# Score products of two attentions: low parts of the keys in full-height tiles with zero rows

## The chip, the cores and the metric

The kernel runs on one core of a Trainium2 chip, as one launch. The metric is the device time of one execution in microseconds. A core has TensorE (PE, matrix products), VectorE (DVE), ScalarE (ACT), GpSimd (POOL) and a queue for transfers (SP).

## What is computed

Two transformer blocks over 512 latent tokens of width 1024 and 256 context tokens, all in float32. Block one has a feed-forward part, then two attentions side by side (a multi-head latent attention, MLA, with 8 heads over all 768 keys, and a neighbourhood attention), a gated merge, and a second feed-forward part. Block two has a chunked mLSTM and a causal window attention side by side, a gated merge, a feed-forward part and a gate. The change concerns the scores of the neighbourhood attention and of the window attention.

Neighbourhood attention: 8 heads of width 64. The 512 queries are a grid of 8 rows by 64 columns, cut into 4 blocks of 16 columns, each block 128 queries. Each query attends in one softmax to the 8 x 32 keys about its block (256 local keys, with a bias table that also masks) and to all 256 context keys:

```python
s_loc = jnp.einsum('bjqhd,bjakhd->bhjqak', q_r, k_b) + bias
s_ctx = jnp.einsum('bjqhd,bkhd->bhjqk', q_r, k_ctx)
p = jax.nn.softmax(jnp.concatenate([s_loc, s_ctx], axis=-1), axis=-1)
```

Window attention: 16 query heads of width 64 share 4 key heads. Each block of 128 queries sees its own and the preceding block of keys (256 columns, 128 for the first block), with a mask and a sink logit per head.

## The kernel before, in words

**Products in parts.** A float32 product is made from operands split into a high part in PE's fast format (float32r) and a low part, the exact rest. A product of weights and activations is high by high, high by low and low by high: three passes of PE. For the two attentions the width of a head is only 64, so both parts of a query stand in one 128-row tile: in `pair_split` (L1135) and in `swa_side` (L1558) the high part has one half of the rows and the low part the other. The high part of the keys, `kh`, stands twice, in both halves. One product of the whole query tile as weights (128 rows) with `kh` gives high by high plus low by high. The second product adds high query by low key. Before, it takes the 64 rows of the query tile that hold the high part as weights and the 64 rows of `kl` that hold this head's low key part; the two heads of a pair lie in the two halves of one `kl` tile. The two products add into the same bank of PSUM.

**Neighbourhood attention** (`na_heads`, L1111): 4 pairs of heads by 4 blocks of queries make 16 units. For a unit, `scores` (L1163) makes for each of two heads four products of 128 queries by 256 keys (local keys and context keys, `kh` and `kl` each), then adds the bias on DVE (L1174), and takes the softmax (L777 on: maximum on DVE, exponential on ACT, reciprocal on DVE, scaling on POOL). `transposes` (L1180) turn the probabilities on PE, and DVE or ACT copies them out of PSUM; `values` (L1192) multiplies them with the values as 64-column weights. The loop (L1213) writes the scores of the next unit between the transposes and the values of the present one. At block 0 of a pair `pair_load` (L1128) starts the transfer of the next pair's queries and keys (`q32`, `k32`, the keys with one buffer); at block 2 `pair_split` makes all the parts for it, `kl` with two buffers.

Beside these 16 units, in steps written alternately by `beside` (L78), runs `mla_out` (L1095): gates (24 products of 512 columns each) and the output product of MLA (12 products), whose result DVE multiplies into `yb` (L1107), which frees the bank.

**Window attention** (`swa_heads`, L1583): 8 pairs of heads by 4 blocks make 32 units. `scores` (L1587) makes for each of two heads two products, 256 columns wide (128 for the first block). The softmax follows with a look-ahead of two units. Beside it runs `swa_side` (L1558): queries, output gates and branch gates (24 products each). The keys are split earlier, in `swa_k` (L1532), beside the mLSTM.

**Order.** The program is written by Tile; a scheduler that works with a simulated timeline fixes the order of instructions on each engine from the order in which they are written, their dependencies and the buffers. On the chip each engine then works through its queue in that order. Weights come by SP in blocks of 512 KB (L94), POOL makes the high part (L103), DVE the low part (L106).

Of the kernel before, what the change touches and what calls it, by code (L numbers as in the profile page):

```python
# [5 lines left out]
F32 = mybir.dt.float32  # L6
# [6 lines left out]
T = 512          # latent tokens  # L13
C = 256          # context tokens
TC = T + C
# [6 lines left out]
# columns of the per-feature vector array  # L22
# [3 lines left out]
# columns of the constant array  # L26
# [5 lines left out]
class Kern:  # L32
    def __init__(self, tc, A, plan):
        self.tc, self.nc, self.A = tc, tc.nc, A
        self.n_dram = 0
        # weights: the order of their use, and how far each step has come
        self.plan, self.log = plan, []
        self.n_use = self.n_split = self.n_dma = 0
        self.w_st, self.w_parts = {}, {}
        self.w_by = "gv"  # the engines of the high and the low part: Pool, vector or scalar  # L40

# [22 lines left out]
    def split(self, hi, lo, src):  # L64
        """hi + lo == src exactly; src in SBUF or PSUM."""
        self.nc.scalar.copy(hi, src)  # L66
        self.nc.vector.tensor_tensor(out=lo, in0=src, in1=hi.bitcast(F32), op=ALU.subtract)
# [10 lines left out]
    def beside(*gens):  # L78
        """Emits generators, given with their numbers of steps, evenly beside one another."""
# [29 lines left out]
    def w(self, name, *idx, c0=0, n=1024, ahead=2):  # L109
        """The next block of weights [128, n], as (hi, lo); splits up to `ahead` blocks more."""  # L110
# [10 lines left out]
    def w_load(self, i):  # L121
        """Starts the load of block i."""
# [4 lines left out]
    def w_ahead(self, i, ahead=2):  # L127
        """Splits up to `ahead` blocks past i, loads up to four more."""
# [14 lines left out]
    def gemm(self, ps, w, xs, c0=0, start=True, stop=True):  # L143
        """ps[128, N] += sum over blocks k of w[:, c0 + 128k ...].T @ xs[k]; xs = (hi, lo) pairs."""
# [8 lines left out]
    def gemms(self, pss, ws, xs):  # L153
        """Several products at once, block k by block k, for an xs that is still being made."""
# [8 lines left out]
    def gemm_tok(self, pss, keys, xs, n, kpc):  # L163
        """Token-major products: pss[i][128 tokens, n] = xs[i]'s tokens @ W; blocks of kpc k each."""
# [27 lines left out]
    def sums_add(self, acc, y, x, g, first, eng):  # L192
        """Per token: adds y^2, (g y) x and (g y)^2 to three sums over features (still one a partition)."""
# [11 lines left out]
    def sums_next(self, put, A, B, C, r):  # L205
        """A = sum over features of (x + r g y)^2, from the sum of x^2 and those above."""
# [6 lines left out]
    def add_normed(self, put, x, y, r, g):  # L213
        """x += y r g."""
# [4 lines left out]
    def next_h(self, put, eng, x, y, r, pre, shift, hh, hl, lo=None):  # L219
        """Parts of h = x r pre + shift. Returns the step that is left for the low part."""  # L220
# [8 lines left out]
    def queue(self):  # L229
        """A function that keeps the instructions given to it in their order, engine by engine."""  # L230
# [12 lines left out]
    def ln_table(self):  # L243
        """Puts a function table in place that has ln and exp."""
# [4 lines left out]
    def ln(self, out, in_, p=None, **kw):  # L249
        """Natural logarithm, after function table p."""  # L250
# [5 lines left out]
    def rstd(self, r, pp, acc, nfeat, pieces=None, p=None):  # L256
        """r = (sum over partitions of acc / nfeat + eps) ** -0.5, on all partitions; function table p."""
# [9 lines left out]
    def setup(self):  # L267
# [22 lines left out]
        # derived per-feature scale columns  # L290
# [5 lines left out]
    def ada_first(self, k, st, put, tp, pp):  # L296
        """Shift, scale of block k of the features, in two steps. Four quarters of the contraction in four
        row groups; a product with ones at the rows of a stream folds them."""
# [19 lines left out]
    def ada_gen(self, tp, pp):  # L318
        """Modulations 2 to 8, one block of features a step, on the vector engine: features on partitions, the
        conditions along the rows. The context takes part in the first three only."""  # L320
# [38 lines left out]
    def ffn1(self):  # L359
# [30 lines left out]
        # shift and scale of one block of features after the other, h, and the first products  # L390
# [44 lines left out]
        def up(f, gh, gl, ss):  # L435
            """Hidden features f of the streams ss."""
# [51 lines left out]
        # the last group: the context's part first, so that its norms run beside the latents' part  # L488
# [7 lines left out]
        def chain(a, b, s):  # L496
            """Residual and next norm of tokens a..b, in steps; ends with the parts of h."""
# [44 lines left out]
        def chain_c():  # L542
            """Residual and next norm of the context, in steps."""
# [50 lines left out]
        # keys and values of the context, and keys of the latents as their features come, beside the norms  # L594
# [13 lines left out]
    def na_kv(self, pp):  # L608
        """Values and keys of the neighbourhood attention to scratch memory. Three steps for three parts of the
        context's keys, one for each block of features of the latents, then the rest."""  # L610
# [39 lines left out]
    def kv_part(self, tp, pp, s):  # L650
        """Compressed keys and values of the latents (s = 0) or the context, normed, in two parts;
        and the rotary key. Three steps of products, then one of the norm."""
# [35 lines left out]
    def rot(self, ps):  # L688
        """Rotary embedding of four 32-row blocks of ps; returns (a, b) with a + b the result."""
# [10 lines left out]
    def mla_proj(self):  # L700
# [10 lines left out]
        # compressed q: gain now, the norm's factor after the next product  # L711
# [19 lines left out]
        # queries  # L731
# [19 lines left out]
        # keys and values  # L751
# [22 lines left out]
    def softmax(self, p, s, tp):  # L774
        """p = softmax along the free axes of s (PSUM)."""
# [14 lines left out]
    def mla_attn(self):  # L790
        """MLA attention, with projections of the other attention beside it."""
# [8 lines left out]
    def cut(self, hi, lo, src):  # L800
        """As split, without the scalar engine; src in SBUF."""
# [3 lines left out]
    def mla_heads(self, tp, pp):  # L805
        """Two heads and 256 queries at a time; the next scores beside the transposes and values."""
# [67 lines left out]
    def na_q(self, pp):  # L874
        """Queries of the neighbourhood attention and gates to scratch memory."""
# [16 lines left out]
    def na_attn(self):  # L892
        """Neighbourhood attention, with the other branch and its gate beside it; then the merge."""
# [88 lines left out]
        def downs(gi, g, a, b):  # L982
            """Tokens a..b of the part of y that group gi brings."""
# [44 lines left out]
        # the last part of y, its norm, the residual, and the next block's h = x * gain (the norm's factor follows  # L1028
        # its products): one half of the tokens beside the products of the other
# [52 lines left out]
    def gate(self, t, w, ps, h, bias=None, r=None):  # L1082
        """t = sigmoid(w.T @ h (r) + 2 bias) as (tanh(z / 2) + 1) / 2."""
# [27 lines left out]
    def na_heads(self, na, on, pp):  # L1111
# [14 lines left out]
        qk = {}  # L1126

# [7 lines left out]
        def pair_split(hp, q, k):  # L1135
            """Per head: queries as high above low part (second head: the other way), keys' high part
            twice; the low parts of both heads' keys."""
            kl = na.tile([128, TC], F32R, tag="kl", name="kl", bufs=2)
            qs, khs = [], []
            for e in range(2):  # L1140
# [7 lines left out]
                nc.vector.tensor_tensor(out=kl[r, :], in0=k[r, :], in1=kh[r, :].bitcast(F32), op=ALU.subtract)  # L1148
                qs.append(qp)
                khs.append(kh)  # L1150
            qk[hp] = qs, khs, kl
# [11 lines left out]
        def scores(hp, j):  # L1163
            qs, kh, kl = qk[hp]
            out = []
            for e in range(2):
                rows = slice(64 * e, 64 * e + 64)
# [3 lines left out]
                for c, sub in ((slice(0, 256), local), (slice(256, 512), lambda t: t[:, T:TC])):  # L1171
                    self.mm(s[:, c], q, sub(kh[e]), stop=False)
                    self.mm(s[:, c], q[rows], sub(kl)[rows], start=False)
# [36 lines left out]
        pair_split(0, *nxt)  # L1210
        cur = scores(0, 0)
        yield 1
        for n, (hp, j) in enumerate(units):  # L1213
# [8 lines left out]
            if j == 2 and hp < 3:  # L1222
                pair_split(hp + 1, *nxt)
            pbs = transposes(cur)
            if n + 1 < len(units):
                cur = scores(*units[n + 1])
# [659 lines left out]
```

## Time and profile before

| | |
|---|---|
| Median of 3 runs | 2535.81 us (2535.79 to 2536.38) |
| Span of the profiled execution, first to last instruction | 2535.5 us |
| Instructions in the span | 31842 |
| PE busy | 2456.4 us (97%), 12360 products |
| DVE busy | 1428.1 us (56%) |
| POOL busy | 818.0 us (32%) |
| ACT busy | 602.6 us (24%) |
| Neighbourhood attention | about 952 to 1092 us of the span |
| Window attention | about 1800 to 1988 us of the span |

The profile is of one execution. Records of PE's products are pipelined: a record's duration includes the way through the array, so consecutive records overlap, and the time that a product holds the engine is read from one start to the next. A share of busy time is a mean over the span. In the view of waits, a line tells which engine and line waited for which, in total, how many times, and the longest.

### The profile page before, as it was taken

How to read it: one execution, taken by the hardware profiler on the slowest of the kernel's cores; microseconds unless marked ns; L12 is line 12 of the kernel's file. 1: busy time of each engine (PE TensorE's matmuls, PEld its weight loads, DVE VectorE, ACT ScalarE, POOL GpSimd, SP SyncE). 2: the span in 40 equal slices, each digit the busy share in tenths (PEclk: the TensorE clock that was granted, in tenths of full speed). 3: DMA queues.
4: the chain of work that ended last, by engine and by line, in shares of the span. 5: the costliest groups of instructions: out<-in, count | busy, mean ns of one | idle time of the engine just before them, and what ended most of it. 6: DMA issues, size and time to landing. Idle time of an engine off the chain costs nothing.

```text
span 2535.5 us, 31842 instructions
## 1 busy us (share of the span) xinstructions
PE 2456.4 (97%) x12360; PEld 2001.6 (79%) x12360; DVE 1428.1 (56%) x2152; ACT 602.6 (24%) x1153; POOL 818.0 (32%) x778
## 2 busy tenths in 40 slices
PE   7999999998999999998999999999999999999997
PEld 4888888987787776776788888777777788888886
DVE  5956555578356447578423338944766545344356
ACT  3210101143223332224111015223533202011023
POOL 2111111336234334355221226725434334212132
PEclk9999999998999999999999999999999999999999
DMA  7444444334322125153332335222222343333332
GB/s 285 158 128 148 128 142 125 126 105 129 131 88 92 55 92 160 61 170 100 95 97 93 101 98 158 84 92 84 80 71 68 117 158 99 100 94 98 99 93 92
DMA packets 97479, 284.67 MB, mean 112 GB/s; under 512 B 10892, under 2 KB 16908, under 8 KB 96176
## 3 DMA queue, kind: packets, MB, share of 16 engines
q1 hardware_dynamic: 87872, 265.86, 32.8%
q10 hardware_dynamic: 9456, 16.78, 2.0%
q8 instruction: 97, 1.59, 0.3%
q14 instruction: 54, 0.44, 0.1%
HBM read 260.32 MB, written 21.50 MB: 111 GB/s over the span
## 4 chain that ended last, share of the span: by engine, by line
PE 85%; DVE 7%; issue 2%; POOL 1%; ACT 1%; DMA 1%; DVEq 0%; POOLq 0%; ACTq 0%
PE mm L59 75%; PE s L59 4%; PE o L59 3%; DVE wlo L106 1%; PE t L853 1%; DVE y L216 1%; PE n L59 1%; PE t L1186 1%; PE q L59 1%; PE pt L1630 1%; DVE acc L190 0%; POOL mqk L1355 0%; DVE t L199 0%; DVE xx L1048 0%; DMA k<-scr 0%
## 5 line engine op out<-in xcount | busy, mean ns | idle before, releaser
L103 POOL TENSOR_SCALAR whi<-wst 128x1024 fp32r<-128x1024 f32 (+4 forms) x387 | 411.7, 1065 | 1334.1 <-PE mm L59 1243.8
L106 DVE TENSOR_TENSOR wlo<-wst,whi 128x1024 fp32r<-128x1024 f32 (+4 forms) x398 | 490.2, 1234 | 288.5 <-POOL whi L103 281.9
L59 PE MATMUL mm<-h2l,whi 128*128 128x512 f32 (+1 forms) x1024 | 354.6, 353 | 3.0 <-DVE h2l L227 3.0
L59 PE MATMUL mm<-h2h,whi 128*128 128x512 f32 (+1 forms) x1024 | 353.4, 354 | 2.4 <-ACT h2h L415 1.9
L59 PE MATMUL mm<-h2h,wlo 128*128 128x512 f32 (+1 forms) x1024 | 353.5, 352 | 2.3 <-DVE wlo L106 2.3
L59 PE MATMUL mm<-gh,whi 128*128 128x512 f32 (+1 forms) x848 | 297.2, 352 | 0.3 <-POOL whi L103 0.3
L59 PE MATMUL mm<-gh,wlo 128*128 128x512 f32 (+1 forms) x848 | 296.4, 351 | 0.7 <-DVE wlo L106 0.7
L59 PE MATMUL mm<-gl,whi 128*128 128x512 f32 (+1 forms) x848 | 296.3, 351 | 0.0
L59 PEld LDWEIGHTS mm<-h2h,wlo 128*128 128x128 f32 x1024 | 194.2, 191 | 30.1 <-DVE wlo L106 3.2
L59 PEld LDWEIGHTS mm<-h2h,whi 128*128 128x128 f32 x1024 | 194.7, 192 | 29.3 <-ACT h2h L415 2.8
L59 PEld LDWEIGHTS mm<-h2l,whi 128*128 128x128 f32 x1024 | 194.5, 192 | 29.5 <-DVE h2l L227 5.0
L59 PEld LDWEIGHTS mm<-gh,wlo 128*128 128x128 f32 x848 | 159.5, 188 | 23.3 <-DVE wlo L106 1.1
L59 PEld LDWEIGHTS mm<-gh,whi 128*128 128x128 f32 x848 | 159.5, 188 | 22.3 <-POOL whi L103 0.8
L59 PEld LDWEIGHTS mm<-gl,whi 128*128 128x128 f32 x848 | 159.7, 188 | 21.7
L59 PE MATMUL mm<-hmh,whi 128*128 128x512 f32 (+1 forms) x432 | 167.1, 398 | 4.0 <-ACT whi L101 4.0
L59 PE MATMUL mm<-hmh,wlo 128*128 128x512 f32 (+1 forms) x432 | 163.0, 390 | 5.4 <-DVE wlo L106 5.4
L59 PE MATMUL mm<-hml,whi 128*128 128x512 f32 (+1 forms) x432 | 161.3, 386 | 0.1
L59 PE MATMUL mm<-hl,whi 128*128 128x512 f32 x352 | 137.9, 392 | 4.3 <-DVE hl L227 4.3
L59 PE MATMUL mm<-hh,wlo 128*128 128x512 f32 x352 | 139.0, 395 | 0.3 <-DVE wlo L106 0.3
L59 PE MATMUL mm<-hh,whi 128*128 128x512 f32 x352 | 137.5, 397 | 0.5 <-POOL whi L103 0.3
L66 ACT CAST gh<-sa 128x512 fp32r<-128x512 f32 (+1 forms) x66 | 36.1, 549 | 276.2 <-DVE sa L456 156.9
L59 PE MATMUL mm<-h4h,whi 128*128 128x512 f32 x256 | 101.2, 395 | 0.0
(414 smaller groups left out, 4429.1 us busy)
## 6 DMA issues: line engine op xcount, KB each, us to landing
wst<-in_f2w SPq DMA_DIRECT2D x60, 512.0 KB, 3.3
ast<-in_w_adaT SPq DMA_DIRECT2D x56, 512.0 KB, 3.3
wst<-in_f1w SPq DMA_DIRECT2D x54, 512.0 KB, 3.4
wst<-in_wup SPq DMA_DIRECT2D x32, 512.0 KB, 3.5
wst<-in_wdn SPq DMA_DIRECT2D x32, 512.0 KB, 3.8
st<-in_w_ada SPq DMA_DIRECT2D x8, 1024.0 KB
wst<-in_wg SPq DMA_DIRECT2D x16, 512.0 KB, 3.2
wst<-in_w2g SPq DMA_DIRECT2D x16, 512.0 KB, 3.6
```

The lines of the kernel that those rows point to most:

```text
L59: ins = self.nc.tensor.matmul(out=out, lhsT=lhsT, rhs=rhs, start=start, stop=stop)
L66: self.nc.scalar.copy(hi, src)
L103: self.nc.gpsimd.tensor_scalar(out=hi[:, :n], in0=st[:, :n], scalar1=1.0, scalar2=0.0, op0=ALU.mult, op1=ALU.add)
L106: e.tensor_tensor(out=lo[:, :n], in0=st[:, :n], in1=hi[:, :n].bitcast(F32), op=ALU.subtract)
L216: put(v.tensor_tensor(out=y, in0=y, in1=r, op=ALU.mult))
L853: nc.tensor.transpose(pt[:, i:i + 128], P[2 * hp + e, 2 * half + q][:, 128 * (2 * c + kk):128 * (2 * c + kk) + 128], self.ident)
L1186: nc.tensor.transpose(pt[:, c], ps[e][:, c], self.ident)
L1630: nc.tensor.transpose(pt[:, kk, e, :], p[:, e, 128 * kk:128 * kk + 128], self.ident)
```

## The change

For both attentions the second score product now uses the whole query tile (128 rows) as weights, as the first does, and the low part of each head's keys stands in a 128-row tile of its own, whose other half is zero. The zero rows face the low part of the query, so that the sum is that of before.

In the neighbourhood attention there are two such tiles, one for each head of a pair (`klz`, one buffer each), whose zero halves are set once by POOL, ahead of the loop; before there were two buffers of one tile for both heads. As the tiles are used by all pairs, the step that makes the low parts is taken out of `pair_split` and is written behind the scores of the next unit, at block 2 of a pair: the scores of block 3 are the last that read the old low parts. In the window attention the low parts have four tiles instead of two, and POOL sets the zero halves in `swa_k`. Comments and docstrings were also taken out.

```diff
         qk = {}
+        klz = [na.tile([128, TC], F32R, name=f"klz{e}") for e in range(2)]
+        for e in range(2):
+            nc.gpsimd.memset(klz[e][64 - 64 * e:128 - 64 * e, :].bitcast(F32), 0.0)
...
         def pair_split(hp, q, k):
-            kl = na.tile([128, TC], F32R, tag="kl", name="kl", bufs=2)
-            qs, khs = [], []
+            qs, khs, src = [], [], {}
...
-                nc.vector.tensor_tensor(out=kl[r, :], in0=k[r, :], in1=kh[r, :].bitcast(F32), op=ALU.subtract)
                 qs.append(qp)
                 khs.append(kh)
-            qk[hp] = qs, khs, kl
+            qk[hp] = qs, khs
+
+            def low():
+                for e in range(2):
+                    r = slice(64 * e, 64 * e + 64)
+                    nc.vector.tensor_tensor(out=klz[e][r, :], in0=k[r, :], in1=khs[e][r, :].bitcast(F32),
+                                            op=ALU.subtract)
+
+            return low
...
         def scores(hp, j):
-            qs, kh, kl = qk[hp]
+            qs, kh = qk[hp]
...
                     self.mm(s[:, c], q, sub(kh[e]), stop=False)
-                    self.mm(s[:, c], q[rows], sub(kl)[rows], start=False)
+                    self.mm(s[:, c], q, sub(klz[e]), start=False)
...
-        pair_split(0, *nxt)
+        pair_split(0, *nxt)()
...
             if j == 2 and hp < 3:
-                pair_split(hp + 1, *nxt)
+                low = pair_split(hp + 1, *nxt)
             pbs = transposes(cur)
             if n + 1 < len(units):
                 cur = scores(*units[n + 1])
+            if j == 2 and hp < 3:
+                low()
             yield 1
             values(hp, j, po, pbs)
...
     def swa_k(self, sw, at, pp, h, r, swk):
...
-            kl = sw.tile([128, T], F32R, name=f"kl{m}")
             for e in range(2):
                 kh = sw.tile([128, T], F32R, name=f"kh{2 * m + e}")
+                kl = sw.tile([128, T], F32R, name=f"kl{2 * m + e}")
                 rws, oth = slice(64 * e, 64 * e + 64), slice(64 - 64 * e, 128 - 64 * e)
+                nc.gpsimd.memset(kl[oth, :].bitcast(F32), 0.0)
                 self.split(kh[rws, :], kl[rws, :], t[rws, :])
                 nc.scalar.copy(kh[oth, :], t[rws, :])
-                swk.append((kh, kl[rws, :]))
+                swk.append((kh, kl))
...
                 self.mm(s[:, e, :w], q[:, c], kh[:, ck], stop=False)
-                rws = slice(64 * (m // 2 % 2), 64 * (m // 2 % 2) + 64)
-                self.mm(s[:, e, :w], q[rws, c], kl[:, ck], start=False)
+                self.mm(s[:, e, :w], q[:, c], kl[:, ck], start=False)
```

## Rows read from the trace of the kernel before

**Rows 1.** The page, its first lines: span, and busy time of engines.

```profile
span 2535.5 us, 31842 instructions
PE 2456.4 (97%) x12360; PEld 2001.6 (79%) x12360; DVE 1428.1 (56%) x2152; ACT 602.6 (24%) x1153; POOL 818.0 (32%) x778
```

**Rows 2.** Busy time by stretch: length, PE, PEld, DVE, ACT, POOL, granted clock, DMA.

```profile
952.00:1092.00 140.00, 138.73 (x740) 99.33 (x738) 87.57 (x163) 38.54 (x90) 49.62 (x62) 0.96 0.38 121
1800.00:1988.00 188.00, 188.00 (x960) 138.37 (x959) 122.81 (x306) 66.71 (x212) 76.54 (x108) 1.00 0.24 74
966.00:975.40 9.40, 9.24 (x23) 6.61 (x24) 9.27 (x15) 2.12 (x5) 8.50 (x8) 0.50 0.63 182
```

**Rows 3.** Waits from 930 to 1100 us: total, times, longest.

```profile
DVE pb L786 <- PE t L1186: 18.0, 10, 4.4
...
PE mm L59 <- DVE yb L1107: 1.2, 1, 1.2
```

**Rows 4.** Waits from 1795 to 1990 us.

```profile
DVE t L1087 <- PE mm L59: 22.2, 13, 2.7
```

**Rows 5.** PE's timeline, a run of eight score products: start, duration, operation, shape.

```profile
1806.71 0.28 PE L59 MATMUL s<-kh,q 128*128 128x256 f32 x1
1806.92 0.38 PE L59 MATMUL s<-kl,q 64*128 64x256 f32 x1
1807.24 0.38 PE L59 MATMUL s<-kh,q 128*128 128x256 f32 x1
...
1809.11 0.51 PE L59 MATMUL mm<-hmh,wlo 128*128 128x512 f32 x1
1809.46 0.40 PE L59 MATMUL mm<-hmh,whi 128*128 128x512 f32 x1
1809.69 0.40 PE L59 MATMUL mm<-hml,whi 128*128 128x512 f32 x1
```

**Rows 6.** PE's timeline, last stage: first and last of 31 products of 256 columns.

```profile
2508.52 0.28 PE L59 MATMUL mm<-h5h,whi 128*128 128x256 f32 x1
...
2511.92 0.28 PE L59 MATMUL mm<-h5h,whi 128*128 128x256 f32 x1
```

**Rows 7.** PE's timeline, MLA scores: two products with the same weights.

```profile
925.93 0.34 PE L59 MATMUL s<-kh,qh 96*128 96x384 f32 x1
926.10 0.33 PE L59 MATMUL s<-kl,qh 96*128 96x384 f32 x1
```

**Rows 8.** PE's timeline, a high-part score beside a product with 64 weight columns.

```profile
1036.87 0.39 PE L59 MATMUL s<-kh,q 128*128 128x256 f32 x1
1037.19 0.54 PE L59 MATMUL o<-pb,nv 128*64 128x128 f32 x5
```

**Rows 9.** PE's timeline, eight transposes and the score behind them.

```profile
1062.49 1.09 PE L1186 MATMUL t<-cst,p 128*128 128x128 f32 x8
1063.34 0.37 PE L59 MATMUL s<-kh,q 128*128 128x256 f32 x1
```

**Rows 10.** Instructions on the score operands, whole span: duration ns min/median/max, starts.

```profile
L59 PEld LDWEIGHTS s<-kh,q x128: 185/187/330, 951.6 to 1980.5; 128*128 128x128 f32 x128
...
L59 PE MATMUL s<-kl,q x128: 282/382/580, 953.3 to 1980.8; 64*128 64x256 f32 x112, 64*128 64x128 f32 x16
...
L1148 DVE TENSOR_TENSOR kl<-k,kh x8: 940/1107/1357, 950.8 to 1025.4; 64x768 fp32r<-64x768 f32 x8
```

**Rows 11.** PE's timeline, a group of four score products of 128 columns.

```profile
1813.84 0.22 PE L59 MATMUL s<-kh,q 128*128 128x128 f32 x1
...
1815.09 0.40 PE L59 MATMUL mm<-hml,whi 128*128 128x512 f32 x1
```

**Rows 12.** DVE's timeline, 956 to 967 us: in brackets idle time before, and releaser.

```profile
963.00 0.55 DVE L1146 CAST kh<-k 64x768 fp32r<-64x768 f32 x1 [6.01 <-DMA k<-scr]
...
965.33 0.69 DVE L1107 TENSOR_TENSOR yb<-yb,mm 128x512 f32<-128x512 f32 x1
```

**Rows 13.** Groups of POOL's instructions, whole span: busy us, mean ns.

```profile
L1324 POOL MEMSET rowp<- 36x2560 f32 x1 | 2.2, 2228 | 0.0
```

More of the change, by code (lines that the diff above doesn't have):

```diff
@@ L1163, in scores @@
         def scores(hp, j):
-            qs, kh, kl = qk[hp]
+            qs, kh = qk[hp]
             out = []
             for e in range(2):
-                rows = slice(64 * e, 64 * e + 64)
                 s = self.bank(pp, "s", 3)
```

## Prediction

> **What bounds the kernel now.** I read the page's busy shares first. TensorE (PE) is busy for 97% of a span of 2535.5 us [rows 1]; the median of the runs is 2535.81 us, so the profiled execution lies 0.3 us below it, and I make the sum against 2535.5 and add 0.3. A busy PE is not a PE at its peak, so I then read the two stretches that the change touches: the neighbourhood attention, 952 to 1092 us, and the window attention, 1800 to 1988 us. In the first PE counts as busy for 138.73 of 140 us, in the second for all of 188; DVE for 87.57 and 122.81 us, which is 63% and 65% [rows 2]. The waits agree: in the first stretch PE's only long wait for another engine's result is 1.2 us, and DVE waits 18.0 us for transposes alone [rows 3]; in the second DVE waits 22.2 us for products [rows 4]. Others wait for PE, so an instruction that PE issues sooner should move the end.
>
> The last view is PE's timeline, read by distances from start to start, as the recorded durations overlap. The reader should see the following in a run of eight score products [rows 5]: high keys, low keys, high keys, low keys, each 256 columns wide, and they start 0.31 to 0.32 us apart (first pair 0.21). Full-array products of the same width in the last stage start 30 steps from 2508.52 to 2511.92, 0.113 us apart [rows 6]. Two differences stand beside one another: the score products change from 128 weight rows to 64 and back, the others don't. MLA's scores change nothing in shape; there two products in a row with the same weights, 384 columns wide, start 0.17 us apart [rows 7], so neither using the weights twice nor adding into one bank costs such a gap. I take the 0.2 us beyond 0.113 as the price of changing shape. It shows in a third place: a product that goes over to 64 weight columns starts 0.32 us after a 256-column score [rows 8], while a score follows transposes without it (eight transposes take 0.85 us, 0.106 each [rows 9]).
>
> **The change part by part.**
> *Low-part products go from 64 to 128 weight rows.* Their number stays 128, of them 112 of 256 columns and 16 of 128 [rows 10]. The price is read from whole groups. In the run of eight the first score starts at 1806.71 and the second product behind the group at 1809.46; a product there takes 0.23 (1809.46 to 1809.69), so the group holds PE for 1809.46 - 0.23 - 1806.71 = 2.52 us [rows 5]. Eight at 0.113 would be 0.90. Saved: 1.62 for four low products, 0.40 each. For 128 columns, a group of four holds it 1815.09 - 0.23 - 1813.84 = 1.02 us [rows 11]; four at 0.106, taking the transposes' step, would be 0.42; saved 0.30 for each low product. Sum: 112 x 0.40 + 16 x 0.30 = 49.6 us. Less where the shape changes anyhow: counted over the timeline of the two stretches, a low product stands directly beside a 64-column product 5 times, and a few low products stand beside one another; together some 7 changes of 0.2, so 1.4. That leaves 48 us of PE time. Bounds for the new step: below, 0.107 us (256 columns at 2.4 GHz, what 0.113 already nearly is), above, 0.17 as in the wider MLA scores; at 0.17 the 256 score products would lose 256 x 0.057 = 15 us of it. I take 0.113, the row with the same width.
>
> *What of it lies on the path.* Nearly all, as PE leads in both stretches, but three pieces come off.
> (a) Start of the neighbourhood attention. DVE waits 6.01 us until 963.00 for the second pair's keys, casts them, and only then, at 965.33, multiplies the product that frees a bank for PE [rows 12]; PE waits 1.2 us for that [rows 3]. That transfer doesn't go faster, so two units' saving ahead of it, 2 x 1.62 = 3.2 us, turns into waiting. DVE loses nothing there, as the low parts come behind it.
> (b) The low parts now have one buffer instead of two. For each of the three later pairs two subtractions (median 1.11 us [rows 10]) must stand between the last scores of a pair and the first of the next. A unit is 140 / 16 = 8.75 us, some 7.1 after the saving; 2.2 us fit. They are queued on DVE in order, with the mask additions and the evacuations behind them, and these hold up softmax and PE's banks. Lower bound 0 (an earlier place of the same work could even relieve the DVE before), upper bound, if the unit before gives no cover, 3 x 2.2 = 6.7. I take 2, nearer the lower end as DVE still has slack. The transfer of the next pair's keys waits for the subtraction that reads the same buffer, on SP's queue with the weight loads behind it; four units lie between, about 28 us, against the longest wait for such keys of 6.01, so I put it at nothing unless the order is bad.
> (c) DVE does the same work in less time: 87.57 of about 115 us and 122.81 of about 164, some 76%. Nothing of it is longer, but its queue is in order, and products wait for its evacuations. Bounds: 0, and 15 us if a third of the saving is lost to it; I take 3, since DVE now waits for PE and not the reverse.
>
> *Zeros.* POOL sets two tiles of 64 x 768 ahead of the first stretch and four of 64 x 512 beside the mLSTM. The set of 36 x 2560 took 2.23 us, 0.87 ns a column [rows 13]; that makes 0.67 us each and 0.45 us each, 3.1 us in all. POOL is busy 49.62 of 140 us in the first stretch [rows 2]; the work hides unless splits of weights stand behind it at a bad place, then up to 3 us. I take 0.
>
> Sum: 48 - 3.2 - 2 - 3 = 40 us; 2535.5 - 40 + 0.3 = 2495.8, about 2496 us.
>
> **A rule against it.** The run of full-array products starts every 0.113 us while a weight load is recorded at 0.187 us [rows 6, 10], so the load lies beside the product before it. The Trainium skill, "TensorE: Matmul & The Clock Gate", section "Part 3: Packing small matmuls", says that a weight load overlaps a running product only when their row groups differ. With every score on all rows, that would expose each load: 0.113 + 0.187 = 0.30 us a step, as before, and the change would bring nothing. This is a rival below; the trace doesn't agree with the rule here. The same skill, "TensorEngine Tiling (Array Packing)", section "Key Properties", says that changing the tiling mode drains the engine, which agrees with the 0.31 us.
>
> **The rivals.**
> 1. *Other engines take up a good part (25%).* The hand-over in (b) and the queue in (c) cost PE waits, and after a wait the clock can fall: from 966 to 975.4 us, behind the 1.2 us wait, the granted clock was 0.50, the 1.2 GHz level, for 9.4 us [rows 2, 3], which costs 4.7 us of work. With the upper bounds 6.7 and 15 in place of 2 and 3 the gain is 48 - 3.2 - 6.7 - 15 = 23; with a new fall of the clock about 19: 2512 to 2517 us. For it: DVE's share rises by 12 points in both stretches. Against: PE doesn't wait for DVE in the second at all.
> 2. *The stretch at half clock goes (10%).* The order in the first stretch shifts so that the wait at 965 us or its sequel vanishes: 48 + 4.7 + 1.2 - 2 = 52 less, 2484 us; without losses at (b) and (c) 2482.
> 3. *Nothing changes (4%).* The gap isn't the shape, or loads show as the rule has it: 2535 us. Against it stand the 0.113 and 0.17 us steps.
> 4. *Slower (3%).* One mechanism: the single low-part buffer at the three hand-overs. If each holds PE for x us and drops the clock as at 966, the cost is 3 (x + 4.7); it eats the 45 us that are left after (a) once x passes 10.3. That takes keys arriving late behind the subtraction that frees their buffer, a 6.01 us wait [rows 12], four casts of 0.55 and two subtractions of 1.11: 10.4 us, just at the point, with no other products to fill PE. PE has products of the other branch beside it, so it is unlikely; with x = 12 it would give 2541 us.
>
> **How the numbers follow.** The forecast of 2496 us, with 2489 to 2506 as its own spread, has 58%; the rivals as above. Faster by over 0.2% (5.1 us, about what a measurement of this kernel can tell from no change): 0.93; within it 0.04; slower 0.03. The range reaches from rival 2 to most of rival 1: 2484 to 2515.
>
> **What would show it.** In the changed profile: no product with 64 weight rows; high and low score products about 0.113 us apart, and a run of eight near 0.9 us; the stretch of the first attention about 20 us shorter, that of the second about 23; PE's busy share near 97% still. Wrong would be: steps of 0.2 us or more inside the groups (price of the step), PE waits on the low-part subtraction at three places (b), DVE above 85% with PE waiting on its evacuations (c), a granted clock of 0.50 at new places, or a stretch elsewhere that grew because instructions were placed in another order.

## The result, and the profile after

The changed kernel takes 2496.86 us in the median (2496.39 to 2496.94, 4 runs), the kernel before 2535.8 us (2533.8 to 2536.38): a ratio of 0.9844, 95% interval 0.9832 to 0.9856. The forecast was 2496.0 us. The total came out as written; its parts didn't all, and the experiments sort them.

The first lines of the page of the changed kernel, which answer to [rows 1]:

```profile
span 2495.1 us, 31838 instructions
PE 2408.0 (97%) x12360; PEld 1985.4 (80%) x12360; DVE 1426.9 (57%) x2152; ACT 599.0 (24%) x1151; POOL 828.7 (33%) x784
```

As many products as before, 48.4 us less PE busy; DVE and ACT are as they were, POOL has 10.7 us more, of which 3.7 are the zeros. PE's timeline of the changed kernel, a run of eight score products (start, duration, operation, shape), which answers to [rows 5]:

```profile
958.35 0.29 PE L59 MATMUL s<-kh,q 128*128 128x256 f32 x1
958.48 0.29 PE L59 MATMUL s<-klz,q 128*128 128x256 f32 x1
...
959.33 0.40 PE L59 MATMUL mm<-h2l,whi 128*128 128x512 f32 x1
959.56 0.40 PE L59 MATMUL mm<-h2h,wlo 128*128 128x512 f32 x1
```

The group holds PE for 959.56 - 0.23 - 958.35 = 0.98 us, where before it was 2.52. So a low product saves 0.385 us; 0.40 was forecast from a step of 0.113, and the step came out at 0.12.

The two profiled spans differ by 40.4 us, the medians by 38.9. Where the 40.4 us lie is read from first starts. The lines of instructions by tile (in ns minimum/median/maximum, then first and last start, in us) of the kernel before, and then of the changed one:

```profile
L59 PE MATMUL s<-kh,q x128: 218/382/580, 951.9 to 1980.5; 128*128 128x256 f32 x112, 128*128 128x128 f32 x16
...
L59 PE MATMUL mm<-onh,whi x32: 394/394/501, 1095.5 to 1116.9; 128*128 128x512 f32 x32
...
L59 PE MATMUL q<-mqk,mqk x32: 270/432/697, 1689.8 to 1776.4; 128*128 128x512 f32 x8, 128*128 128x384 f32 x8, 128*128 128x256 f32 x8, 128*128 128x128 f32 x8
...
L59 PE MATMUL mm<-sbh,whi x64: 388/394/506, 1991.3 to 2073.2; 128*128 128x512 f32 x64
```

```profile
L59 PE MATMUL s<-kh,q x128: 220/283/415, 949.9 to 1940.5; 128*128 128x256 f32 x112, 128*128 128x128 f32 x16
...
L59 PE MATMUL mm<-onh,whi x32: 394/394/502, 1079.5 to 1100.9; 128*128 128x512 f32 x32
...
L59 PE MATMUL q<-mqk,mqk x32: 270/432/697, 1671.8 to 1758.4; 128*128 128x512 f32 x8, 128*128 128x384 f32 x8, 128*128 128x256 f32 x8, 128*128 128x128 f32 x8
...
L59 PE MATMUL mm<-sbh,whi x64: 388/394/505, 1950.9 to 2032.8; 128*128 128x512 f32 x64
```

From the first score of the neighbourhood attention to the first product behind it (`onh`) is the **first stretch**: 1095.5 - 951.9 = 143.6 us before, 129.6 after, 14.0 less. From the mLSTM's first product (`mqk`) to the first product behind the window attention (`sbh`) is the **second stretch**: 301.5 before, 279.1 after, 22.4 less. The other 4.0 us lie outside of both.

The waits of the changed kernel (total, times, longest) in the first stretch:

```profile
DVE kh L1148 <- DMA k<-scr: 16.0, 3, 9.3
...
PE mm L59 <- DVE yb L1107: 6.7, 1, 6.7
...
PE o L59 <- DVE pb L786: 3.7, 3, 3.0
```

and about the second:

```profile
DVE t L1087 <- PE mm L59: 10.6, 11, 1.9
```

In the first stretch, the wait of 1.2 us in [rows 3] has become 6.7, and a second one of 3.0 us is new. In the second, DVE still waits for PE, 10.6 us in place of the 22.2 of [rows 4]. DVE's timeline shows where the first stretch's waits come from (in brackets idle time before, and releaser):

```profile
963.57 0.55 DVE L1148 CAST kh<-k 64x768 fp32r<-64x768 f32 x1 [9.29 <-DMA k<-scr]
...
989.23 0.55 DVE L1148 CAST kh<-k 64x768 fp32r<-64x768 f32 x1 [4.82 <-DMA k<-scr]
```

and PE's, what follows from them:

```profile
966.70 0.77 PE L59 MATMUL mm<-omh,whi 128*128 128x512 f32 x1 [6.74 <-DVE yb L1107]
...
994.34 0.90 PE L59 MATMUL o<-pb,nv 128*64 128x128 f32 x5 [3.04 <-DVE pb L786]
```

DVE stands at the cast of keys that haven't come: of the second pair until 963.57, as in [rows 12], and of the third until 989.23. (In the kernel before DVE also stood 4.57 us at the third pair's keys, and PE didn't wait for what stood behind them.) Behind the casts on its queue are the multiplication and the copy that PE needs. Behind both waits the granted clock was 0.50, the 1.2 GHz level, for 3.2 and 6.2 us, together the 9.4 us of before [rows 2]:

```profile
966.60:969.80 3.20, 3.10 (x7) 2.51 (x8) 3.14 (x6) 1.36 (x3) 2.58 (x3) 0.50 0.39 132
994.30:1000.50 6.20, 6.16 (x28) 5.32 (x29) 6.14 (x14) 2.03 (x5) 2.05 (x3) 0.50 0.18 57
```

(busy time by stretch; columns as in [rows 2]).

### The profile page after: what moved, and what is told of

Read it like the earlier page. It is cut to its first block, busy times and chain, and to the rows that moved or that the text cites. A ratio compares the mean times of both kernels' runs of the same rounds, so it can differ in the third digit from the quotient of the medians.

```text
span 2495.1 us, 31838 instructions
## 1 busy us (share of the span) xinstructions
PE 2408.0 (97%) x12360; PEld 1985.4 (80%) x12360; DVE 1426.9 (57%) x2152; ACT 599.0 (24%) x1151; POOL 828.7 (33%) x784
## 4 chain that ended last, share of the span: by engine, by line
PE 47%; DVE 5%; issue 2%; ACT 1%; POOL 1%; DMA 0%; DVEq 0%; ACTq 0%; POOLq 0%
PE mm L59 44%; DVE wlo L106 1%; PE n L59 1%; PE o L59 1%; PE s L59 1%; PE q L59 1%; PE pt L1641 1%; POOL whi L103 0%; DVE xx L1048 0%; DVE mqk L1367 0%; ACT L245 0%; DVE hml L1267 0%; POOL mqk L1365 0%; DVE y L216 0%; DVE xz L1721 0%
## 5 line engine op out<-in xcount | busy, mean ns | idle before, releaser
L59 PEld LDWEIGHTS mm<-gh,whi 128*128 128x128 f32 x848 | 159.5, 188 | 22.4 <-POOL whi L103 0.8
```

What stands on the lines that cost most here:

```text
L59: ins = self.nc.tensor.matmul(out=out, lhsT=lhsT, rhs=rhs, start=start, stop=stop)
```

## The experiments

The table has the median, the ratio to the kernel before in the same set of runs, and from each profile the two stretches and the rest of the span, in us.

| kernel | median | ratio, 95% interval | first | second | rest |
|---|---|---|---|---|---|
| before | 2535.8 | | 143.6 | 301.5 | 2090.4 |
| changed | 2496.86 | 0.9844 (0.9832 to 0.9856) | 129.6 | 279.1 | 2086.4 |
| E1 window part only | 2511.68 | 0.9901 (0.9884 to 0.9918) | 145.2 | 279.2 | 2086.7 |
| E2 neighbourhood part only | 2520.6 | 0.9936 (0.9919 to 0.9953) | 126.4 | 301.5 | 2090.7 |
| E3 mirrored order | 2517.5 | 0.9921 (0.9906 to 0.9936) | 135.3 | 290.9 | 2092.0 |
| E4 keys twice | 2497.04 | 0.9842 (0.9827 to 0.9857) | 126.8 | 279.2 | 2087.4 |
| E5 early keys | 2501.27 | 0.9862 (0.9848 to 0.9875) | 130.6 | 279.1 | 2089.5 |
| E6 early keys, queries | 2493.89 | 0.9832 (0.9818 to 0.9845) | 123.6 | 279.1 | 2090.5 |
| E7 before, early keys | 2538.76 | 1.0013 (1.0004 to 1.0022) | 145.8 | 301.5 | 2088.7 |
| E8 low parts made twice | 2493.64 | 0.9831 (0.9818 to 0.9845) | 126.4 | 279.1 | 2085.9 |
| E9 one pair loaded | 2486.53 | 0.9796 (0.9779 to 0.9812) | 116.6 | 279.2 | 2090.1 |
| E10 pairs by ScalarE's queue | 2493.11 | 0.9825 (0.9810 to 0.9839) | 122.1 | 279.1 | 2089.3 |
| E11 the same, early | 2494.01 | 0.9828 (0.9813 to 0.9843) | 124.1 | 279.2 | 2090.3 |
| E12 values by ScalarE's queue | 2493.47 | 0.9824 (0.9809 to 0.9838) | 124.9 | 279.1 | 2088.1 |

Two things stand out before any single run. The second stretch has three values, for the three ways of its scores, and is the same to 0.1 us within each. The rest of the span goes from 2085.9 to 2092.0 with no relation to what was edited, though apart from POOL's two sets of zeros for `klz` (0.73 us each) and the issue of early loads no edit lies there; so of the first profile's 40.4 us the 4.0 outside the stretches lie within that scatter.

**E1, the window part alone** (`swa_k` and `swa_heads` of the changed kernel in the kernel before):

```diff
-                swk.append((kh, kl[rws, :]))
+                swk.append((kh, kl))
...
-                self.mm(s[:, e, :w], q[rws, c], kl[:, ck], start=False)
+                self.mm(s[:, e, :w], q[:, c], kl[:, ck], start=False)
```

> Only the window attention's part of the change. Theory (each low product loses two changes of shape, 0.40 us at 256 columns and 0.30 at 128, and the window attention has no other loss): 22 to 24 us less than before, about 2512 to 2514 us, with the neighbourhood stretch as before. Rival (the gain in the window attention depends on the first attention's new order, or the 4 us that the changed profile gains outside the two stretches belong to the window part): 18 us or less, or 26 us and more.

2511.68 us, 24 less than before: the theory holds. In the profile 22.3 us of it lie in the second stretch, as in the changed kernel, and the first is no shorter.

**E2, the neighbourhood part alone** (the changed kernel with `swa_k` and `swa_heads` as before):

```diff
-                swk.append((kh, kl))
+                swk.append((kh, kl[rws, :]))
```

> Only the neighbourhood attention's part. Theory (25 us of PE time saved there, about 11 given back to waits for the pairs' keys): 13 to 16 us less than before, about 2520 to 2523 us, with PE waits of about 6.7 us and 3 us in that stretch. Rival (the two parts share the loss, each part alone gives its full 24): 2512 us or less.

2520.6 us, 15 less: the time is the theory's, and by the medians the two parts add up (24 + 15 = 39). PE waits 7.1 us at the same place. But the second wait, which the theory counted in, is at most 0.5 us here, and the first stretch is 126.4 us, 3.2 shorter than in the changed kernel, though the same lines of the program make it. DVE stands 2.26 us at the third pair's keys, in place of 4.82; so the 3.0 us wait of the changed kernel is a matter of how late those keys land.

**E3, mirrored order.** The kernel before, its 64-row products untouched, in the order high, low, low, high:

```diff
-                for c, sub in ((slice(0, 256), local), (slice(256, 512), lambda t: t[:, T:TC])):
-                    self.mm(s[:, c], q, sub(kh[e]), stop=False)
-                    self.mm(s[:, c], q[rows], sub(kl)[rows], start=False)
+                ctx = lambda t: t[:, T:TC]
+                self.mm(s[:, 0:256], q, local(kh[e]), stop=False)
+                self.mm(s[:, 0:256], q[rows], local(kl)[rows], start=False)
+                self.mm(s[:, 256:512], q[rows], ctx(kl)[rows], stop=False)
+                self.mm(s[:, 256:512], q, ctx(kh[e]), start=False)
```

(and in the same way for the two heads of a unit of the window attention).

> The kernel before, with 64-row low products as they were, in mirrored order: high, low, low, high instead of high, low, high, low, so two changes of shape in a group of four instead of four. Theory (the price is the change of shape, 0.2 us each): a group of four takes about 0.4 us less, 64 groups some 25 us of PE time, of which the neighbourhood part loses some to the wait for keys: 2512 to 2520 us. Rival (a product with 64 weight rows is dear by itself, whatever stands beside it): no change, 2533 to 2538 us.

2517.5 us, 18 less. PE's timeline of this kernel:

```profile
1814.74 0.28 PE L59 MATMUL s<-kh,q 128*128 128x256 f32 x1
1814.95 0.50 PE L59 MATMUL s<-kl,q 64*128 64x256 f32 x2
1815.38 0.39 PE L59 MATMUL s<-kh,q 128*128 128x256 f32 x1
1815.61 0.39 PE L59 MATMUL mm<-hmh,whi 128*128 128x512 f32 x1
```

A group of four takes 1815.61 - 1814.74 = 0.87 us, with two changes of shape. With four it took half of 2.52, so 1.26, and in the changed kernel, with none, half of 0.98, so 0.49. Each pair of changes costs 0.38 to 0.39 us, 0.19 for one, with products of 256 columns. As E3 has as many 64-row products as the kernel before, the price is shown to be that of the change of shape, and not of the 64 rows.

The records of the weight loads (PEld) show where the time goes. In the kernel before, each load in the run of eight starts with its own product, those of [rows 5] at 1806.92 and 1807.24:

```profile
1806.92 0.18 PEld L59 LDWEIGHTS s<-kl,q 64*128 64x128 f32 x1 [0.25 <-issue]
1807.23 0.19 PEld L59 LDWEIGHTS s<-kh,q 128*128 128x128 f32 x1
```

In the changed kernel it starts with the product before, so that the load for the product at 958.48 lies beside the one that starts at 958.35:

```profile
958.36 0.19 PEld L59 LDWEIGHTS s<-klz,q 128*128 128x128 f32 x1
958.48 0.19 PEld L59 LDWEIGHTS s<-kh,q 128*128 128x128 f32 x1
```

Counted over the trace of the kernel before, all 200 score products that directly follow a product of another shape have a load that starts with them, to 0.005 us. In the changed kernel 252 follow one of the same shape, and 249 of these have their load earlier, by 0.12 us in the median. So a change of shape costs about one weight load (0.18 to 0.19 us) that no longer lies beside the product before. The Trainium skill, "TensorEngine Tiling (Array Packing)", section "Key Properties", says that a change of the tiling mode drains the engine; a load that waits for the product before is in keeping with that, and the price here is 0.19 us.

**E4, two buffers for the pairs' keys** in the changed kernel:

```diff
-            k = na.tile([128, TC], F32, tag="k32", name="k32")
+            k = na.tile([128, TC], F32, tag="k32", name="k32", bufs=2)
```

> The changed kernel, with two buffers for the keys of a pair as they come from memory instead of one. Theory (the two PE waits in the neighbourhood stretch, 6.7 and 3.0 us, and the half clock behind them, come from DVE standing at a cast whose keys are late because their only buffer was freed late): both go, 10 to 14 us less than the changed kernel, 2483 to 2488 us. Rival (DVE is simply full there, and the wait moves to its next instruction): within 3 us of the changed kernel, 2494 to 2499 us.

2497.04 us: the theory falls as far as the time goes. The second wait is gone, the first stays:

```profile
PE mm L59 <- DVE yb L1107: 6.5, 1, 6.5
```

DVE still stands 9.0 us at the second pair's keys. With the second buffer their transfer was issued at 949.15 in place of 951.10, and they landed at 962.89 in place of 963.57: the buffer was not what made them late. The third pair's keys were issued at 966.27 in place of 983.34, and for that wait the theory was right.

**E5 and E6, earlier transfers.** In E5 the second pair's keys are loaded ahead of the biases and values, in E6 its queries too (both with two key buffers). E6's edit, beside the second buffer:

```diff
         nxt = pair_load(0)
+        nxt1 = pair_load(1)
         bias_load(0)
...
-                nxt = pair_load(hp + 1)
+                nxt = pair_load(hp + 1) if hp else nxt1
```

> The changed kernel with two key buffers, and the transfer of the second pair's keys written ahead of the biases and values instead of behind the first scores. Theory (the PE wait of about 6.5 us at the start of the neighbourhood stretch is DVE standing at the cast of keys that wait behind the biases and values on the queue, and the half clock follows from it): the wait shrinks to under 1 us, 6 to 9 us less than the changed kernel, 2488 to 2491 us. Rival (the transfers at that place are as much as the memory queue can carry, so the biases or values become late instead): within 2 us of the changed kernel, 2495 to 2499 us.

> As the run before, with the second pair's queries moved ahead too. Theory: if DVE or POOL stand at the queries once the keys are there, this is another 1 to 3 us less than with early keys alone; if the keys alone were late, the same within 1.5 us. Rival (a buffer of the shared tag is held longer, so that the gates' first step waits): slower than early keys alone by 2 us or more.

E5 takes 2501.27 us; neither theory nor rival had that. It is not shown to be slower than the changed kernel: the intervals overlap, and in the profiles only 1.0 us of the difference lies in the first stretch. The wait at the cast is gone, but POOL now stands at the queries (its timeline), and PE at the transposes of the probabilities that POOL scales (the waits):

```profile
969.24 1.81 POOL L1152 TENSOR_SCALAR q<-q 64x512 fp32r<-64x512 f32 x2 [9.77 <-DMA q<-scr]
```

```profile
PE t L1201 <- POOL p L782: 8.3, 1, 8.3
```

E6 takes that away, 2493.89 us, 7 less than E5, where 1 to 3 were expected. The wait moves to the low parts of the second pair. Its keys are there, but the subtractions stand on DVE's queue behind the casts of the third pair's keys, which haven't come (DVE's timeline, then the waits):

```profile
978.73 0.55 DVE L1148 CAST kh<-k 64x768 fp32r<-64x768 f32 x1 [7.82 <-DMA k<-scr]
...
980.22 0.95 DVE L1157 TENSOR_TENSOR klz<-k,kh 64x768 fp32r<-64x768 f32 x1
```

```profile
PE s L59 <- DVE klz L1157: 5.9, 2, 5.0
```

**E7, early keys in the kernel before** (the edit of E5: two key buffers, the second pair's keys ahead of the biases).

> The kernel before with the same early keys. Theory (there the same wait was 1.2 us, with half the clock for 9.4 us behind it, 4.7 us of work): 3 to 6 us less than before, 2530 to 2533 us. Rival (the fall of the clock has another cause than the wait): 1 us less at most.

2538.76 us, 3 more than before: the theory falls. Here too the wait only moved, to POOL's scaling (3.7 us), and the half clock came with it: 0.63 in the mean from 970 to 980 us.

**E8, the low parts twice.** The changed kernel with the hand-over's subtractions written twice for the three later pairs:

```diff
             if j == 2 and hp < 3:
                 low()
+                low()
```

> The changed kernel with the low parts of the three later pairs subtracted twice, so six subtractions more on DVE, 6.6 us of its time, at the hand-overs. Theory (the hand-over is covered by the unit beside it): 0 to 2 us more than the changed kernel, 2496 to 2499 us. Rival (the hand-over lies on the path, as its upper bound of 6.7 us had it): 5 to 8 us more, 2502 to 2505 us.

2493.64 us, no slower; by the profiles it is 3.2 us shorter in the first stretch, which has the large wait but not the second one:

```profile
PE mm L59 <- DVE yb L1107: 7.6, 1, 7.6
```

So the hand-over is covered, as the theory had it: E2 and E4, which have the first wait alone too, have first stretches of 126.4 and 126.8 us with the subtractions made once, and E8 has 126.4. That it came out shorter than the changed kernel is not explained by the edit; the order of instructions moved, and DVE no longer stood at the third pair's keys.

**E9, one pair's data for all.** The changed kernel with one load of queries and keys:

```diff
-            q = self.np_.tile([128, T], F32, tag="t", name="q32", bufs=3)
+            q = na.tile([128, T], F32, tag="q32", name="q32")
...
             if j == 0 and hp < 3:
-                nxt = pair_load(hp + 1)
+                pass
```

> The changed kernel without the transfers of the three later pairs' queries and keys: all pairs use those of the first pair (left out: the loads of queries and keys of heads 2 to 7, so those heads' scores are of heads 0 and 1). All arithmetic stays. Theory (at the start of the neighbourhood stretch PE waits for what stands behind late transfers of pairs; each earlier load only handed the wait to the next late one): no PE wait over 1 us from 950 to 1000 us, the stretch 7 to 10 us shorter than in the changed kernel, 2486 to 2490 us. Rival (DVE and POOL have too much to do there, transfers or not): PE waits of 5 us or more remain, 2493 us or more.

2486.53 us, within the theory's range. No wait of PE in the stretch is longer than 0.5 us, and the clock stays whole. Busy time by stretch (columns as in [rows 2]), of the changed kernel and then of this one:

```profile
950.00:1070.00 120.00, 110.22 (x706) 89.25 (x706) 82.20 (x155) 36.13 (x85) 47.68 (x59) 0.94 0.39 120
```

```profile
950.00:1070.00 120.00, 118.66 (x786) 95.02 (x785) 91.17 (x170) 39.86 (x92) 48.12 (x61) 1.00 0.43 137
```

DVE is busy for 91.17 us there, 9 more than in the changed kernel in the same time, and PE isn't held up: it was not DVE's load that made PE wait, it was the transfers. (E9 also takes the queries out of the buffers that they share with the gates; no run separates that.) The first stretch is 13.0 us shorter than in the changed kernel, more than the 7 to 10 expected; 9.8 are the two waits, and the half clock (9.4 us at 0.50, 4.7 of work) is more than the rest.

**E10 to E12, another queue.** E10: two key buffers, and the pairs' loads issued by ScalarE's queue. E11: the same, the second pair early. E12: E6, with the local values issued by ScalarE's queue.

```diff
-            nc.sync.dma_start(out=q, in_=self.naq[hp])
-            nc.sync.dma_start(out=k, in_=self.nak[hp])
+            nc.scalar.dma_start(out=q, in_=self.naq[hp])
+            nc.scalar.dma_start(out=k, in_=self.nak[hp])
```

> The changed kernel with two key buffers and the transfers of the pairs' queries and keys issued by ScalarE's queue, in place of SP's, where they stand behind biases and values. Theory (the order on SP's queue makes them late): the wait at 966 us falls below 2 us and the time by 4 to 8 us against the changed kernel, 2489 to 2493 us. Rival (the transfers all share the same engines and are late by volume, or ScalarE's own work stands ahead of them): within 2 us of it, or slower, 2495 to 2501 us.

> As the run before, and the second pair's load written ahead of the biases and values. Theory: as early keys and queries on SP's queue or better, 2487 to 2494 us. Rival (later pairs' loads are now what is late, by volume): 2493 to 2498 us.

> Early keys and queries on SP's queue with two key buffers, and the local values loaded by ScalarE's queue, so that later keys don't stand behind them on SP's. Theory: the 5 us wait at the hand-over to the second pair's low parts, which came from the third pair's late keys, shrinks to under 2 us: 2487 to 2491 us. Rival (volume, not order): 2493 to 2497 us.

2493.11, 2494.01 and 2493.47 us. In E10 the wait at 966 us is gone, as the theory had it, but PE waits 3.5 us for POOL at 969, and the time lies at the edge of the theory's range. E11 lies in the rival's range, at the edge of the theory's. In E12 the rival's time came, but not by its reason: the hand-over no longer waits, and PE waits for ScalarE instead. The longest waits of the three, in order:

```profile
PE t L1194 <- POOL p L782: 3.9, 2, 3.5
```

```profile
PE s L59 <- ACT p L780: 4.8, 1, 4.8
```

```profile
PE mm L59 <- ACT ga L1092: 7.9, 1, 7.9
```

In E11 and E12 it is no late data that ScalarE stands at. Its instructions stand behind the issues of loads on its own queue: in E11 behind one of keys, issued at 986.17, in E12 behind eight of values (ScalarE's timeline of E12):

```profile
944.66 16.98 ACTq L1164 DMA_DIRECT2D nv<-scr  x8
961.74 0.69 ACT L1092 ACTIVATE ga<-mm,hb 128x512 f32<-128x512 f32 x1 [16.50 <-DMA nv<-scr]
```

The intervals of E6, E8 and E10 to E12 overlap one another and that of the changed kernel, so no full version is shown to be faster than it; E10 has the lowest median and the shortest first stretch of them.

## Why the prediction was right, and where it wasn't

**The price of a change of shape: right.** 1.62 us for a run of eight were forecast, 1.54 measured; E3 shows the cause by halving the changes, and the loads' records show what it consists of. The rule of the Trainium skill ("TensorE: Matmul & The Clock Gate", "Part 3: Packing small matmuls"), weighed in the prediction, that loads overlap only between different row groups, would have kept steps of 0.30 us; this trace has 0.12 on all rows, and the loads that don't overlap are those behind a change of shape: the step of 0.31 us before is such a load (0.19) behind a product of 0.12.

**The window attention: right.** About 23 us were forecast for its stretch, 22.4 measured, and 24 by E1's time. The queue on DVE cost nothing there; of the 3 us in (c) nothing was needed in this stretch.

**The neighbourhood attention: short.** About 20 us were forecast, 14.0 measured. The groups' own saving is 32 x 0.77 = 24.6. Step (a), the wait for the second pair's keys, was rightly placed but mis-sized: 3.2 us were to turn into waiting, 5.5 did (6.7 against 1.2). PE came to the wait 3.0 us earlier, counted from the first score, as the step said; the keys came 2.6 us later, counted in the same way (963.57 - 949.86 = 13.7 against 963.0 - 951.9 = 11.1), and "that transfer doesn't go faster" left open that it could be slower: from issue to cast it took 12.5 us (951.10 to 963.57) in place of 9.9 (953.12 to 963.00).

In (b) the hand-over itself was given 2 us and cost nothing: PE has no wait of over 0.2 us for `klz` in the changed kernel, and E8 agrees. But the transfer of the next pair's keys, which the step put "at nothing unless the order is bad", cost the second wait, 3.0 us. The step took four units, about 28 us, to lie between the subtraction that frees the buffer and the next keys' use. On the queues, as the scheduler ordered them, it was far less (DVE and SP, kernel before):

```profile
971.55 1.33 DVE L1148 TENSOR_TENSOR kl<-k,kh 64x768 fp32r<-64x768 f32 x1
...
975.24 0.38 SPq L1132 DMA_DIRECT2D k<-scr  x1
...
983.80 0.55 DVE L1146 CAST kh<-k 64x768 fp32r<-64x768 f32 x1 [4.57 <-DMA k<-scr]
```

and in the changed kernel:

```profile
980.35 0.95 DVE L1157 TENSOR_TENSOR klz<-k,kh 64x768 fp32r<-64x768 f32 x1
...
983.34 0.33 SPq L1135 DMA_DIRECT2D k<-scr  x1
...
989.23 0.55 DVE L1148 CAST kh<-k 64x768 fp32r<-64x768 f32 x1 [4.82 <-DMA k<-scr]
```

The hand-over moved the subtraction's end from 972.9 to 981.3, and the transfer's issue with it; DVE reached the cast 3.1 us after that end (989.23 - 4.82 - 981.30). A second buffer takes the wait away (E4), but in E2 and E8 it is absent with one, so the order counts as much.

Of the 24.6 some 1.0 go off for low products that stood beside another change of shape (5 changes of 0.19, by a count of the changes in both traces). Less 5.5 and 3.0 that leaves 15.1; 14.0 was measured. The half clock takes nothing off, as it lasts 9.4 us before and after.

**The total: right in part by chance.** The two stretches gave 36.4 of the forecast 40 us; 4.0 more came from the rest of the span, whose scatter over these kernels is as large. By the medians the gain is 38.9. The prediction put the profiled execution 0.3 us below the median by comparing a span with a device time; in the later runs the device time is about 1.8 us above the span (2496.89 against 2495.1), so by that the profiled execution before lay some 1.5 us above its median.

**The rivals.** The first one (other engines take a good part) came true in the first stretch alone and by another cause: PE did wait for DVE, and the clock fell, but DVE was waiting for memory, not full. For it stood a rise of DVE's share by 12 points in both stretches; the prediction's own figures give 14 and 10, and the first rose from 62% to 68%. The slower one needed 10.3 us at each of three hand-overs; the largest wait there was 3.0.

**What stays open.** E9 gains 27.0 us in the first stretch on the kernel before; 23.6 for the groups and 5.9 for the wait and half clock there would be 29.5. The missing 2.5 us weren't traced, nor was the scatter of the rest, nor why the second pair's transfer took longer in the changed kernel. One rival cure wasn't tried: to leave the transfers as they are and put the multiplication that PE waits for ahead of the casts on DVE's queue.

## What to carry to other kernels

Read the step from one product to the next in every group of small products: where weights change between 64 and 128 rows from product to product, 0.19 us each is lost (at 256 columns), and zero rows that keep one shape, or an order that puts like shapes together, take it back. Before counting such a gain in full, look in each stage for the transfer that ends last: PE's saving ahead of it only becomes a longer wait. When a buffer comes free is set by where its last reader stands on its engine's queue, not by where that is written in the program. A wait of an engine that serves PE in order is worth tracing to its own releaser, since what seemed a busy DVE here was a DVE that stood at late keys.

## What the runs showed of the hardware that was not expected

A weight load lies beside the product before it as long as the shape stays (0.12 us from product to product), and starts only with its own product where the shape changes, in all 200 cases of the kernel before.

Moving a late transfer forward only moved the wait: in E5, E6, E11 and E12 PE waited 8.3, 5.0, 4.8 and 7.9 us in the same 40 us. In E5 and E6 POOL and DVE stood at the next late transfer; in E11 and E12 ScalarE stood at the issue of loads that had been put on its queue. Only without the later pairs' transfers (E9) did the wait go. Six subtractions more on DVE in a stretch where it is busy two thirds of the time (E8) cost nothing that could be measured, while the order in which the same work was issued moved the first stretch by 3 to 6 us in the profiles (E8 and E6 against the changed kernel), though no time beyond its interval.
